# A two-layer trunk on one core: the first feed-forward block by seven half-size products, with the S5 tables made in small pieces

## The chip, the cores and the metric

The kernel runs on one core of a Trainium2 chip. The metric is the device time of one execution in microseconds (us), the median of several runs. Engines are named as in the profile: PE multiplies matrices (PEld loads its weights), DVE does elementwise work, ACT does functions and copies, POOL is the fourth compute engine and also issues transfers of its own, SP only issues transfers.

## What is computed

Two layers over 544 tokens (512 of a prompt and 32 of samples) of width 1024. Each layer is a gated feed-forward block, a set of four mixers (SSD, RWKV, S5, pool) between an input and an output projection, and a second gated feed-forward block; a last norm follows.

```python
def _layer(x, pos0, st, p):
    x = x + 0.5 * _swiglu(_rmsnorm(x, p['norm_ffn1']), p['ffn1_in'], p['ffn1_out'])
    u = _rmsnorm(x, p['norm_mix']) @ p['w_in']
    ...                                    # four mixers on slices of u
    x = x + y @ p['w_out']
    x = x + 0.5 * _swiglu(_rmsnorm(x, p['norm_ffn2']), p['ffn2_in'], p['ffn2_out'])
```

The S5 mixer needs `a_bar = exp(lam*delta)`, its powers, and products of these powers with `b` and `c`; they depend on the weights alone and are called the S5 tables here.

## The kernel before

**Layout.** x lies in SBUF as eight tiles of 128 channels by 544 tokens, and is worked on in two halves of 272 tokens. Weights come from DRAM in chunks of eight 128x128 blocks (`fetch`, tile `wraw`, four buffers). Every fp32 value is split in a rounded high part and the rest, so a product of one weight block with one tile is six matmuls of 272 columns (`mm3`, L832 to L834: high by high, high by low, low by high, for two halves). The weight split is `parts` (L816 the cast on ACT, L819 the subtraction on DVE); its results `whi` and `wlo` have three buffers of four blocks each.

**The feed-forward block in two forms.** There are 22 hidden tiles m. In `ffn`, used for the first block of layer 0 alone, each hidden tile takes 16 weight blocks, that is 96 matmuls (`inph`); the output projection of a group of hidden tiles follows (`outph`, groups of 8, 8 and 6). In `ffs`, used for the three other blocks, the first four hidden tiles go the same way (`plain`); the other 18 go by `quad(m)`, which makes a 2x2 by 2x2 block product with seven instead of eight products of half-size (Winograd's scheme: 7 x 12 = 84 matmuls, L975 and L976). For this `forms` makes seven combinations of the normalized x once in a block, during `plain(1)` to `plain(3)`, and each quad makes its weight combinations t1 to t4 (L979, DVE), splits seven of them (`form`, tiles `xh0..7` and `xl0..7`; three of the seven low parts are made by a copy with the sign turned on ACT and an accumulating transfer issued by POOL, L818), and takes the four results out of PSUM (tiles `pm`, all four banks). Between quads lie two output tiles of the group before (`out`, PSUM tile `pd`, two buffers, evicted into x by L1007).

**The S5 tables.** `do_prep` runs `s5_prep` for both layers, as a generator whose next piece `ffn` asks for after each hidden tile from the third on. It has six pieces for each layer: two of small operations on 16 columns and one for each four of 16 S5 groups. A piece of four groups makes CA (three DVE operations, L593), GB (three), four transposes (L664) and four fp32 matmuls recorded as eight (L670) on PE with a PSUM bank of `pm`, two ACT copies, sines and cosines (`sincos`, L599 to L606) and RHO (two POOL operations), and writes the results to DRAM with 13 transfers on SP's queue (eight of them L673). The parameters come with one transfer on ACT's queue, tied behind the last weight fetch (`issue_after`).

**Order.** The program is traced in the order of the code, and a scheduler at compile time then puts each engine's instructions in a fixed order, the earliest traced first among those that it holds ready. Work traced later can so fill gaps of work traced earlier. In `ffn` weights are fetched by ACT's queue, in `ffs` by SP's.

**Constants.** One tile `cst` with all constants is loaded at the start by SP, and `mat`, weights of the mixers, by ACT at the start of each layer (L1199).

Of the kernel before, what the change touches and what calls it, by code (L numbers as in the profile page):

```python
# [7 lines left out]
def build_consts():  # L8
    c={}
    I=np.arange  # L10
    p=I(128)
# [93 lines left out]
class Mix:  # L105
# [6 lines left out]
    def c(s,n,rows=128):  # L112
        o,k=CC[n]; return s.cst[0:rows,o:o+k]
# [3 lines left out]
    def load_consts(s,cst):  # L117
        s.cst=s.const.tile([128,CONST.shape[1]],F32,name="cst"); s.nc.sync.dma_start(s.cst,cst)
# [463 lines left out]
    def s5_prep(s,par,name,tp):  # L582
# [5 lines left out]
        tl=lambda n,a: tp.tile([128]+a,F32,name=n)  # L588
# [8 lines left out]
        def sincos(E,y,sn,cs,k):  # L597
# [30 lines left out]
        bbr=tl("bbr",[16,16]); bbi=tl("bbi",[16,16]); t3=tl("t3",[16,16]); bbS=tl("bbS",[16,16])  # L628
        qrb=qr[:,:,None].to_broadcast([128,16,16]); qib=qi[:,:,None].to_broadcast([128,16,16])
        TT(V,bbr,br,qrb,M); TT(V,t3,bi,qib,M); TT(V,bbr,bbr,t3,SB)  # L630
        TT(V,bbi,bi,qrb,M); TT(V,t3,br,qib,M); TT(V,bbi,bbi,t3,AD)
        A.copy(bbS[0:64],bbr[0:64]); A.copy(bbS[64:128],bbi[64:128])

        A1=tl("A1",[9,16]); A2=tl("A2",[9,16])
        V.tensor_copy(A1[0:64],pr[0:64]); V.tensor_copy(A1[64:128],pi[64:128])
        V.tensor_copy(A2[0:64],pi[0:64]); V.tensor_copy(A2[64:128],pr[64:128])
        sg=s.c('sgn')
# [4 lines left out]
        ab4=tl("ab4",[32]); V.tensor_copy(ab4[:,0:16],pr[:,4,:]); V.tensor_scalar(ab4[:,16:32],pi[:,4,:],sg,-1.0,op0=M,op1=M)  # L642
# [8 lines left out]
        for g0 in range(0,16,4):  # L651
# [10 lines left out]
            GT=tl("GT",[4,128])  # L662
            ps=s.bank(); pv=ps.rearrange("p (g q) -> p g q",g=4)
# [5 lines left out]
            ps=s.bank(); pv=ps[0:16,:].rearrange("p (g q) -> p g q",g=4)  # L669
# [4 lines left out]
            ph=tl("ph",[4,64]); kk=tl("kk5",[4,64]); SN=tl("SN",[4,64]); CS=tl("CSt",[4,64])  # L674
# [3 lines left out]
            V.tensor_scalar(SN,SN,sg,None,op0=M)  # L678
# [87 lines left out]
GROUPS=[list(range(0,8)),list(range(8,16)),list(range(16,22))]  # L766
# [18 lines left out]
class Kern(Mix):  # L785
    def __init__(s,tc,nc,ctx,io):
        Mix.__init__(s,tc,nc,ctx)
        s.io=io
        s.fi=0
        s.wp=s.P("wp",3); s.xhl=s.P("xhl",1); s.hole=ExitStack()  # L790
        s.wi=0; s.lo=nc.vector; s.dq=nc.scalar
        s.psm=s.P("psm",4,space=bass.MemoryType.PSUM,reuse_waits="tile"); s.psd=s.P("psd",2,space=bass.MemoryType.PSUM,reuse_waits="tile")
# [86 lines left out]
    def ffn(s,st,gnext,bg=iter(())):  # L879
        nc=s.nc  # L880
        with s.tc.tile_pool(name="ffh",bufs=12,reuse_waits="tile") as hp, s.tc.tile_pool(name="fft",bufs=2,reuse_waits="tile") as tp, s.tc.tile_pool(name="ffr",bufs=1,reuse_waits="tile") as rp:
            r=None; hs={}
            v2=lambda t: t.rearrange("p (a b) -> p a b",a=2)
            def inph(m):
                nonlocal r
                pg=s.psd.tile([128,2,512],F32,name="pd")
# [292 lines left out]
    def run(s):  # L1179
# [15 lines left out]
        st={}  # L1195
# [112 lines left out]
```

## Time and profile before

| | |
|---|---|
| median of 3 runs | 2282.89 us (2279.74 to 2290.09) |
| profiled execution, time | 2284.78 us |
| profiled execution, span | 2283.0 us |
| PE busy | 2182.9 us, 96% |
| DVE, ACT, POOL busy | 65%, 48%, 24% |

The profile is that of one execution. A line names the engine, the source line, the tiles written and read, and the duration; what stands in brackets is how long the engine had been idle before and what ended that. The stages follow one another: first feed-forward block of layer 0 to 444 us, mixers to 785, second block to 1163, first block of layer 1 to 1545, mixers to 1889, second block to the end.

### The profile page before, as it was taken

Reading aid. Unit: us, or ns where it says so; the run is one execution under the profiler, and the core shown is the slowest. Engines: PE = TensorE matmul, PEld = TensorE weight load, DVE = VectorE, ACT = ScalarE, POOL = GpSimd, SP = SyncE. Lnnn points to the kernel's source line nnn. Section 1 sums busy time; section 2 is a strip of 40 time slices with the busy share of each in tenths; the row PEclk is TensorE's granted clock in tenths of the full one; section 3 lists DMA queues with packets and bytes.
Section 4 is the critical chain, followed back from the end, with each engine's and each line's share of the span. In section 5 each row is a group of like instructions: output and inputs, shape, how many; then the busy total and the mean of one; then the engine's idle time right before and its main releaser. Section 6 shows DMA issues by size and latency. Waiting matters only on the chain. (4 is left out here: it accounts for less than half of the span.)

```text
span 2283.0 us, 42463 instructions
## 1 busy us (share of the span) xinstructions
PE 2182.9 (96%) x16838; PEld 2124.7 (93%) x16838; DVE 1486.7 (65%) x2757; ACT 1093.6 (48%) x2008; POOL 556.6 (24%) x636
## 2 busy tenths in 40 slices
PE   7899999989899999999999999999899999999997
PEld 7899999988789999999999999999777999999997
DVE  7848633458876677666567666653877667766664
ACT  5324322445435465555455555544554446555542
POOL 3311201334322231111122111114433133111112
PEclk9999999999999999999999999999999999999999
DMA  4343522443322265555437555544432144656551
GB/s 178 114 121 110 147 91 86 150 148 103 101 69 88 86 153 153 140 152 134 116 94 174 133 148 144 139 132 155 118 102 74 36 131 115 174 130 159 129 145 51
DMA packets 142198, 281.20 MB, mean 123 GB/s; under 512 B 36144, under 2 KB 60720, under 8 KB 141872
## 3 DMA queue, kind: packets, MB, share of 16 engines
q1 hardware_dynamic: 91520, 150.77, 20.2%
q0 software_dynamic: 26784, 49.16, 12.6%
q10 hardware_dynamic: 23696, 78.56, 10.5%
q8 instruction: 132, 2.16, 0.4%
q14 instruction: 66, 0.54, 0.1%
HBM read 201.07 MB, written 28.22 MB: 100 GB/s over the span
## 5 line engine op out<-in xcount | busy, mean ns | idle before, releaser
L832 PE MATMUL pd<-xh,whi 128*128 128x272 f32 (+1 forms) x1984 | 548.3, 295 | 17.7 <-ACT whi L816 10.7
L833 PE MATMUL pd<-xl,whi 128*128 128x272 f32 (+1 forms) x1984 | 553.9, 295 | 3.6 <-DVE xl L850 3.5
L816 ACT CAST whi<-wraw 128x512 fp32r<-128x512 f32 x428 | 263.6, 618 | 519.0 <-PE pd L833 405.0
L834 PE MATMUL pd<-xh,wlo 128*128 128x272 f32 (+1 forms) x1984 | 423.7, 294 | 17.0 <-DVE wlo L819 15.2
L832 PEld LDWEIGHTS pd<-xh,whi 128*128 128x128 f32 x1984 | 381.7, 192 | 23.7 <-ACT whi L816 11.9
L975 PE MATMUL pm<-AH,xh 128*128 128x272 f32 x1512 | 393.6, 288 | 5.9 <-DVE e L979 4.2
L975 PE MATMUL pm<-AL,xh 128*128 128x272 f32 x1512 | 393.2, 288 | 0.0
L833 PEld LDWEIGHTS pd<-xl,whi 128*128 128x128 f32 x1984 | 382.5, 193 | 8.2 <-DVE xl L850 5.1
L832 PE MATMUL pd<-hh,whi 128*128 128x272 f32 x1396 | 376.4, 288 | 0.0
L833 PE MATMUL pd<-hl,whi 128*128 128x272 f32 x1396 | 375.9, 288 | 0.0
L834 PEld LDWEIGHTS pd<-xh,wlo 128*128 128x128 f32 x1984 | 322.4, 192 | 22.5 <-DVE wlo L819 18.5
L819 DVE TENSOR_TENSOR wlo<-wraw,whi 128x512 fp32r<-128x512 f32 x328 | 239.0, 729 | 119.8 <-ACT whi L816 113.4
L975 PEld LDWEIGHTS pm<-AH,xh 128*128 128x128 f32 x1512 | 284.4, 188 | 7.2 <-DVE e L979 4.9
L834 PE MATMUL pd<-hh,wlo 128*128 128x272 f32 x1396 | 288.7, 288 | 0.0
L975 PEld LDWEIGHTS pm<-AL,xh 128*128 128x128 f32 x1512 | 284.6, 188 | 0.0
L833 PEld LDWEIGHTS pd<-hl,whi 128*128 128x128 f32 x1396 | 262.8, 188 | 0.0
L832 PEld LDWEIGHTS pd<-hh,whi 128*128 128x128 f32 x1396 | 262.7, 188 | 0.0
L818 POOL DMA_DIRECT2D xl<-wraw x108 | 93.7, 867 | 654.8 <-DVE s L979 443.4
L976 PE MATMUL pm<-AH,xl 128*128 128x272 f32 x1512 | 252.1, 288 | 0.2 <-DMA xl<-sqa 0.2
L834 PEld LDWEIGHTS pd<-hh,wlo 128*128 128x128 f32 x1396 | 219.1, 188 | 0.0
L976 PEld LDWEIGHTS pm<-AH,xl 128*128 128x128 f32 x1512 | 214.9, 188 | 0.4 <-DMA xl<-sqa 0.4
L819 POOL TENSOR_TENSOR wlo<-wraw,whi 128x512 fp32r<-128x512 f32 x100 | 137.0, 1375 | 158.8 <-ACT whi L816 129.9
(516 smaller groups left out, 3316.1 us busy)
## 6 DMA issues: line engine op xcount, KB each, us to landing
wraw<-in_w SPq DMA_DIRECT2D x198, 512.0 KB, 4.0
wraw<-in_w ACTq DMA_DIRECT2D x124, 512.0 KB, 3.4
xl<-wraw POOLq DMA_DIRECT2D x108, 256.0 KB, 3.6
xl<-sqa POOLq DMA_DIRECT2D x54, 256.0 KB, 3.3
AL<-ss POOLq DMA_DIRECT2D x24, 272.0 KB, 5.2
xd<-x SPq DMA_DIRECT2D x16, 272.0 KB, 2.9
x<-xd SPq DMA_DIRECT2D x16, 272.0 KB, 4.7
x<-in_x SPq DMA_DIRECT2D x8, 272.0 KB, 6.9
```

The lines of the kernel that those rows point to most:

```text
L816: nc.scalar.copy(hi,x)
L818: nc.scalar.mul(lo,x,-1.0); nc.gpsimd.dma_start(lo,x,accum_op=OP.add)
L819: else: s.lo.tensor_tensor(lo,x,hi.bitcast(F32),op=OP.subtract)
L832: nc.tensor.matmul(p,wh,rh[:,a:b],start=(n==0),stop=False)
L833: nc.tensor.matmul(p,wh,rl[:,a:b],start=False,stop=False)
L834: for p,a,b in o: nc.tensor.matmul(p,wl,rh[:,a:b],start=False,stop=(n==K-1))
L975: for t in F[j]: nc.tensor.matmul(o,wh[:,j,:],t[:,f,:],start=first and j==0 and t is F[j][0],stop=False,skip_group_check=True)
L976: for j in range(4): nc.tensor.matmul(o,wl[:,j,:],F[j][0][:,f,:],start=False,stop=j==3,skip_group_check=True)
```

## The change

The function `ffn` is dropped, and the first block goes by `ffs` too, so that 18 of its 22 hidden tiles are quads. `s5_prep` is cut into 15 pieces for each layer; layer 0's tables are made in the first block, layer 1's in the second block of layer 0, one piece asked for after each quad. In a piece, small multiplications and copies go from DVE to ACT, the PSUM tile is of `pd`, and several tiles lie in buffers of the feed-forward block (`ss`). The constants are in two tiles: a small one loaded at the start, and a large one that is loaded, like `mat`, at the start of each layer's mixers, into memory that the feed-forward block has used for its `gt`, `s2` and `e`. The hidden tiles have 8 buffers instead of 9 in `ffs` (12 in `ffn`). x lies on the other side of SBUF in the first block.

```diff
+    c['nsg']=-c['sgn']
+    c['hpi']=np.full((128,1),math.pi/2,np.float32)
...
-            V.scalar_tensor_tensor(k,y,-1.0,y,op0=M,op1=OP.max)
-            E.tensor_scalar(k,k,-1.0,math.pi/2,op0=M,op1=AD)
-            A.activation(cs,k,AF.Sin)
+            A.activation(k,y,AF.Abs)
+            A.activation(cs,k,AF.Sin,scale=-1.0,bias=s.c('hpi'))
...
+        yield dst
...
-        V.tensor_scalar(P1,A1,sg,None,op0=M); V.tensor_scalar(P2,A2,-1.0,None,op0=M)
+        A.mul(P1,A1,sg); A.mul(P2,A2,-1.0)
         for d in range(8):
-            V.tensor_copy(Q1[:,7-d,:],A1[:,d,:]); V.tensor_scalar(Q2[:,7-d,:],A2[:,d,:],sg,-1.0,op0=M,op1=M)
+            A.copy(Q1[:,7-d,:],A1[:,d,:]); A.mul(Q2[:,7-d,:],A2[:,d,:],ng)
...
-            GB=tl("GB",[4,8,16]); u=t4[:,:,0:8,:]
+            yield dst
+            GB=half(("p (g s c) -> p g s c",dict(g=4,s=8))); u=t4[:,:,0:8,:]
...
-            ps=s.bank(); pv=ps.rearrange("p (g q) -> p g q",g=4)
+            pp=s.psd.tile([128,2,512],F32,name="pd"); pv=pp[:,0,:].rearrange("p (g q) -> p g q",g=4)
...
-            ph=tl("ph",[4,64]); kk=tl("kk5",[4,64]); SN=tl("SN",[4,64]); CS=tl("CSt",[4,64])
+            yield dst
+            pk,sc=[half(("p (a g k) -> p a g k",dict(a=2,g=4))) for _ in range(2)]; ...
...
-            V.tensor_scalar(SN,SN,sg,None,op0=M)
+            A.mul(SN,SN,sg)
...
-    def ffn(s,st,gnext,bg=iter(())):
...
-    def ffs(s,st,gcur,gnext):
+    def ffs(s,st,gcur,gnext,bg=iter(())):
...
-            ...; hp=pool("ffh",9); tp=pool("fft",2); rp=pool("ffr",1)
+            ...; tp=pool("fft",2); rp=pool("ffr",1); hp=pool("ffh",8)
...
-                for k in range(KD): s.mm3(pg,st[k],k,KD,s.HALF)
-                if r is None: r=s.rstd(st['acc'],rp,tp,'gt')
+                for k in range(KD):
+                    if k not in st: st[k]=s.split(k,s.x[k],s.v(gcur,k))
+                    s.mm3(pg,st[k],k,KD,s.HALF)
+                if 'acc' not in st:
+                    with s.tc.tile_pool(name="ini",...) as ip: s.squares(st,ip); r=s.rstd(st['acc'],rp,tp,'gt')
+                elif r is None: r=s.rstd(st['acc'],rp,tp,'gt')
...
-                    quad(m)
+                    quad(m); next(bg,None)
                     for M in out_order(gi,q): out(SGROUPS[gi-1],M,False)
+            for _ in bg: pass
...
+        mx=s.hole=ExitStack(); rk=ExitStack(); mc=pool(mx,"mxc")
+        s.load_consts(1,mc); s.mat=mc.tile([128,1024],F32,name="mat"); nc.sync.dma_start(s.mat,io['mat'][l][:,0:1024])
         for k in range(KD): nc.sync.dma_start(xd[k],s.x[k])
-        s.xctx.close(); s.hole.close()
+        s.xctx.close()
...
-        s.open_x()
+        s.open_x("right")
...
-        s.load_consts(io['cst'])
-        s.mat=s.const.tile([128,1024],F32,name="mat"); ...
+        s.load_consts(0,s.const)
...
-            nc.scalar.dma_start(s.mat,io['mat'][l][:,0:1024])
...
-            st=s.ffn(st,'nm',s.do_prep()) if l==0 else s.ffs(st,'nf1','nm')
+            st=s.ffs(st,'nf1','nm',s.do_prep(0) if l==0 else iter(()))
...
-        r=s.ffs(st,'nf2','nf1'); s.norm_tile=old
+        r=s.ffs(st,'nf2','nf1',s.do_prep(1)); s.norm_tile=old
```

## Rows read from the trace of the kernel before

**Rows 1.** The page, part 1: busy times, shares of the span, instructions.
```profile
PE 2182.9 (96%) x16838; PEld 2124.7 (93%) x16838; DVE 1486.7 (65%) x2757; ACT 1093.6 (48%) x2008; POOL 556.6 (24%) x636
```

**Rows 2.** DVE's timeline (start us, us, line, operation): evictions that mark pitches.
```profile
390.23 0.73 DVE L897 TENSOR_TENSOR gt<-pd,rsq_r 128x544 f32<-128x544 f32 x1 [1.92 <-PE pd L834]
402.29 0.72 DVE L897 TENSOR_TENSOR gt<-pd,rsq_r 128x544 f32<-128x544 f32 x1 [1.92 <-PE pd L834]
...
1109.10 0.44 DVE L979 TENSOR_TENSOR e<-pm,e 128x272 f32<-128x272 f32 x1 [0.73 <-PE pm L976]
1119.67 0.44 DVE L979 TENSOR_TENSOR e<-pm,e 128x272 f32<-128x272 f32 x1 [0.39 <-PE pm L976]
```

**Rows 3.** DVE's timeline: the last eviction of each stage into x.
```profile
444.47 0.72 DVE L912 SCALAR_TENSOR_TENSOR x<-pd,x 128x544 f32<-128x544 f32 x1 [2.19 <-PE pd L834]
785.68 0.72 DVE L1122 TENSOR_TENSOR x<-pd,x 128x544 f32<-128x544 f32 x1
1163.28 0.72 DVE L1007 SCALAR_TENSOR_TENSOR x<-pd,x 128x544 f32<-128x544 f32 x1 [0.40 <-PE pd L834]
1544.77 0.72 DVE L1007 SCALAR_TENSOR_TENSOR x<-pd,x 128x544 f32<-128x544 f32 x1 [2.19 <-PE pd L834]
1889.43 0.72 DVE L1122 TENSOR_TENSOR x<-pd,x 128x544 f32<-128x544 f32 x1
```

**Rows 4.** PE's timeline: the first block's second hidden tile begins.
```profile
34.24 0.36 PE L832 MATMUL pd<-xh,whi 128*128 128x272 f32 x1 [1.91 <-DVE gt L897]
```

**Rows 5.** Stretches of the first block: busy time (count) of PE, PEld, DVE, ACT, POOL; clock; DMA.
```profile
25.00:125.00 100.00, 92.13 (x688) 89.55 (x687) 80.23 (x194) 39.44 (x72) 28.81 (x25) 0.96 0.38 118
175.00:275.00 100.00, 99.39 (x786) 97.19 (x786) 80.60 (x194) 40.15 (x71) 23.24 (x22) 1.00 0.43 133
300.00:400.00 100.00, 100.00 (x799) 100.00 (x798) 33.90 (x51) 26.56 (x43) 12.21 (x9) 1.00 0.26 87
55.00:65.00 10.00, 8.15 (x53) 7.93 (x52) 10.00 (x35) 3.93 (x7) 2.69 (x2) 0.83 0.39 125
```

**Rows 6.** What PE waited for from 25 to 126 us: total, times, longest.
```profile
PE pd L834 <- DVE wlo L819: 6.0, 4, 2.1
```

**Rows 7.** PE's timeline around the tables' transposes and matmuls of four groups.
```profile
87.18 0.60 PE L664 MATMUL pm<-cst,GB 128*128 128x128 f32 x4
87.71 1.05 PE L670 MATMUL pm<-CA,bbS 128*16 128x128 f32 x8
88.68 0.39 PE L832 MATMUL pd<-xh,whi 128*128 128x272 f32 x1
```

**Rows 8.** PE's waits, 862 to 1163 us (all) and 1230 to 1550 us (all).
```profile
PE pm L975 <- DVE e L979: 0.8, 1, 0.8
...
PE pm L975 <- DVE e L979: 2.2, 1, 2.2
```

**Rows 9.** Stretches of the second block of layer 0, columns as in rows 5.
```profile
829.00:845.50 16.50, 16.50 (x133) 16.50 (x133) 16.00 (x26) 13.59 (x26) 5.58 (x6) 1.00 0.83 201
862.00:1079.00 217.00, 216.24 (x1722) 216.01 (x1721) 145.09 (x253) 114.71 (x211) 33.68 (x39) 1.00 0.56 143
```

**Rows 10.** ACT's timeline in that block: a cast just after a quad's first product.
```profile
1057.20 0.62 ACT L816 CAST xh<-sq 128x512 fp32r<-128x512 f32 x1 [0.16 <-PE pm L975]
```

**Rows 11.** Table operations: timeline at 97 us; durations (min/median/max ns) of three.
```profile
97.78 1.40 POOL L903 TENSOR_TENSOR hl<-s,hh 128x544 fp32r<-128x544 f32 x1
97.88 1.91 DVE L593 TENSOR_TENSOR CA<-CA,t 128x576 f32<-128x576 f32 x1
...
L593 DVE TENSOR_TENSOR CA<-s5par,P x8: 744/1916/1925, 58.8 to 262.4; 128x576 f32<-128x576 f32 x8
L606 ACT ACTIVATE cs<-kr x4: 198/200/218, 44.2 to 205.4; 128x16 f32<-128x16 f32 x4
L673 SPq DMA_DIRECT2D s5d<-KZ x64: 313/424/1725, 98.3 to 279.4; - x64
```

**Rows 12.** The accumulating transfers of the quads: durations of issue on POOL.
```profile
L818 POOL DMA_DIRECT2D xl<-wraw x108: 855/862/1022, 839.1 to 2219.8; - x108
```

More of the change, by code (lines that the diff above doesn't have):

```diff
@@ L45, in build_consts @@
     c['rcnt']=(1.0/np.minimum(I(16)[None,None,:]+1,w[:,:,None])).astype(np.float32).reshape(128,32)
-    cols={}; o=0; arr=[]
+    c['nsg']=-c['sgn']
+    c['hpi']=np.full((128,1),math.pi/2,np.float32)
+    cols={}; arr=[[],[]]
     for n,a in c.items():
-        cols[n]=(o,a.shape[1]); o+=a.shape[1]; arr.append(a)
-    return np.ascontiguousarray(np.concatenate(arr,1)),cols
+        j=0 if n in ('idn','one','kap','sgn','nsg','hpi') else 1
+        cols[n]=(j,sum(b.shape[1] for b in arr[j]),a.shape[1]); arr[j].append(a)
+    return [np.ascontiguousarray(np.concatenate(a,1)) for a in arr],cols
 F32=mybir.dt.float32; F32R=mybir.dt.float32r
@@ L112, in c @@
     def c(s,n,rows=128):
-        o,k=CC[n]; return s.cst[0:rows,o:o+k]
+        j,o,k=CC[n]; return s.cst[j][0:rows,o:o+k]
     def v(s,n,j=0,k=1):
@@ L587, in s5_prep @@
         dst=s.dram.tile([128,O['END']],F32,name=name)
-        tl=lambda n,a: tp.tile([128]+a,F32,name=n)
+        tl=lambda n,a,tag=None: tp.tile([128]+a,F32,name=n,tag=tag or n)
+        half=lambda a: s.ntp.tile([128,T],F32,name="ss",bufs=2)[:,0:512].rearrange(a[0],**a[1])
         pt=tl("s5par",[1072])
@@ L673, in s5_prep @@
                 nc.sync.dma_start(dst[si*16:si*16+16,g0*128:g0*128+512].rearrange("p (g q) -> p g q",g=4),KZ[:,:,128-16*si:256-16*si])
-            ph=tl("ph",[4,64]); kk=tl("kk5",[4,64]); SN=tl("SN",[4,64]); CS=tl("CSt",[4,64])
+            yield dst
+            pk,sc=[half(("p (a g k) -> p a g k",dict(a=2,g=4))) for _ in range(2)]; ph,kk,SN,CS=pk[:,0],pk[:,1],sc[:,0],sc[:,1]
             kap=s.c('kap')[:,None,:].to_broadcast([128,4,64])
@@ L1191, in run @@
         s.pre.append(s.fetch(1))
-        s.load_consts(io['cst'])
-        s.mat=s.const.tile([128,1024],F32,name="mat"); s.om=s.const.tile([128,12],F32,name="om")
+        s.load_consts(0,s.const)
+        s.om=s.const.tile([128,12],F32,name="om")
         s.vec=s.vecs[0]
@@ L1207, in run, with do_prep @@
             st=s.ffn2(l,st)
-        s.xctx.close(); s.hole.close()
-    def do_prep(s):
+        s.xctx.close()
+    def do_prep(s,l):
         with s.tc.tile_pool(name="s5prep",bufs=1,side="right",reuse_waits="tile") as tp:
-            for l in range(2):
-                for s.prep[l] in s.s5_prep(s.io['s5par'][l],f"s5d{l}",tp): yield
+            for s.prep[l] in s.s5_prep(s.io['s5par'][l],f"s5d{l}",tp): yield
     def ffn2(s,l,st):
@@ L1238, in ffs @@
             for h in SGROUPS[-1]: out.append(blk(wo,h,M))
-    def ffn(wi,wo):
-        def inb(m):
-            for k in range(8): out.append(blk(wi,k,m))
-            for k in range(8): out.append(blk(wi,k,m+NH))
-        for gi,G in enumerate(GROUPS):
-            for m in (G if gi==0 else G[1:]): inb(m)
-            if gi<2: inb(GROUPS[gi+1][0])
-            for M in range(8):
-                for m in G: out.append(blk(wo,m,M))
-    (ffs if l else ffn)(i['ffn1_in'][l],i['ffn1_out'][l])
+    ffs(i['ffn1_in'][l],i['ffn1_out'][l])
     W=i['w_in'][l]
```

75 lines of the change are left out of this document (19 added, 56 removed).

## The prediction

> **What bounds the kernel now.** I read the page's first part, then the stages, then each stage's waits. PE is busy for 96% of the span, no other engine for more than 65% [rows 1]. That is a share over stages, so I looked for the pitch of the work. In the first block's later part one hidden tile's half is evicted at 390.23 us and the next tile's at 402.29, so a plain hidden tile takes 12.06 us for 96 matmuls, 0.1256 us each; where two quads follow each other without output tiles between them, their evictions stand 10.57 us apart, which is 84 matmuls at 0.1258 us [rows 2]. Both pitches are those of matmuls with no gap. The blocks are thus bounded by the number of matmuls, with exceptions in the first block: from 25 to 125 us PE is busy for 92.13 of 100 us, and it had 688 matmuls where a quiet stretch of the same block has 799 [rows 5]. There DVE is full (10.00 of 10 us from 55 to 65 us), the granted clock falls to 0.83 of full speed, a mixture of 2.4 and 1.2 GHz, after PE had waited [rows 5], and PE waits for the low parts of weights, four times, 6.0 us in all [rows 6]. What fills DVE there are the S5 tables.
>
> **The change part by part.** The profiled execution took 2284.78 us with a span of 2283.0; the median of the runs is 2282.89. I make the sum on the trace and take it off the median, which is 1.9 us below the profiled time.
>
> *Seven products.* 18 hidden tiles go from 12.06 to 10.57 us: 18 x 1.49 = **-26.8 us** [rows 2]. The output projection has the same 1056 matmuls before and after. This is on the path, since PE has no gap at either pitch.
>
> *What the tables cost in the old first block.* PE begins the second hidden tile at 34.24 us [rows 4] and the last eviction is at 444.47 [rows 3], 410.2 us. The matmuls in it are 22 x 96 + 1056 - 96 = 3072, at 0.1256 us 385.8 us. The tables' own PE work of four groups lasts from 87.18 to 88.68 us, 1.5 us [rows 7], and there are eight such, 12.0 us. The remainder is 410.2 - 385.8 - 12.0 = 12.4 us. The 6.0 us of waits are half of it [rows 6]; a clock of 0.83 over 10 us is another 1.7 us, and the like once more around 100 us. All of it goes with the old arrangement: **-12.4 us**. The 12.0 us of table work stay, half of them moved from the first block to the second: 0.
>
> *What the form with seven products costs by itself.* A block of this form has 4 x 96 + 18 x 84 + 1056 = 2952 matmuls, at 0.1256 us 370.8 us. The second block of layer 0 takes 1163.28 - 785.68 = 377.6 us, the first of layer 1 381.5 us [rows 3], so 6.8 and 10.7 us more. Most of that is the norm at the start, which the old first block has too, before 34.24 us; after the start I find waits of 0.8 us in one and of 2.2 us in the other [rows 8]. I take **+3 us**, between 0.8 and 6.
>
> *The tables between the quads.* This is the term that no row shows. The demand first. While layer 1's tables were made, DVE was busy 80.60 us in 100; without tables 33.90 [rows 5]. The tables of a layer thus cost DVE about 47 us. In the quads' stretch DVE is busy 145.09 us of 217, ACT 114.71 [rows 9]; a quad and two output tiles last 10.57 + 6.03 = 16.6 us, so DVE is free for 5.5 us of each and ACT for 7.8. There are 16 such pairs in a block, 88 us of free DVE time for 47 us of tables, in pieces of some 2 to 4 us. Less than 47 will be wanted: of each layer's operations on 16 columns some 18 go to ACT at about 0.2 us (the like of L606's 198 ns), 3.6 us, and ACT has 16 x 7.8 = 125 us [rows 9, 11].
>
> Then the slack. In the old block the low parts of weights have three buffers, each good for 24 matmuls or 3.0 us, so one is made at most 6.0 us before its use. In a quad the cast at 1057.20 us waited for PE to leave the tile that the quad's first product had read [rows 10]. There are eight such tiles and seven forms in a quad, so this cast is for the second product of the *next* quad, which begins 16.6 us later. A piece of 2 to 4 us on DVE does not reach PE through the forms. The tight ones are the evictions of `pm`: a bank is needed again two products, 3.0 us, after its product ends. An eviction can stand behind one table operation of 0.7 to 1.9 us, not behind a whole piece.
>
> First what the row shows on the length of these operations: the CA operations took 744 ns at best and 1916 at the median, and one of 1.91 us at 97.88 us stands beside a POOL subtraction of 1.40 us that began 0.1 us before it [rows 11]. The Trainium skill (SBUF — State Buffer, SBUF: two separate sides) has the port pair that VectorE and GpSimd share as an exclusive lock: whoever comes first holds it for its whole instruction. The trace agrees, 1.91 us against 0.744. By that rule the tables would be cheaper in quads, where the subtraction and the last product are DVE's own: 4 x (1.916 - 0.744) = 4.7 us of each layer's 47 would go for the first CA operation alone. The sum below does not use it.
>
> The price: at best 0 (below that, the remainder of 12.4 us has already been taken off in full). At worst as much for each piece as in the old block, 12.4 us over 12 pieces, 1.03 us, times 30 new pieces: 31 us. I take **+7 us**, near the lower end, because the lead is nearly three times as long and the old loss fell almost wholly on layer 0: PE was 99.39% busy while layer 1's tables were made [rows 5]. Part of it I expect around the fourth hidden tile, where DVE is already busy 16.00 of 16.5 us [rows 9] and the first pieces come.
>
> *Queues.* The tables' 53 transfers of a layer now share SP's queue with the weight chunks, which ACT's queue had in the old first block. Eight of them at 0.42 us stand in a row [rows 11], 3.4 us in which a chunk can wait; the lead of a quad hides that. Without it, 8 x 3.4 = 27 us; I take 0. The parameters' load was tied behind a weight fetch on ACT's queue and is so no longer; it can only come earlier. SP's load of the large constants waits for tiles last read by the last quad; behind it on SP stand x's stores, which wait for the last output tiles (36 us of matmuls) anyway: 0.
>
> *Start.* The norm's matmuls come after the eighth instead of the ninth weight block, so the factor is known up to 1.5 us sooner, and PE had waited 1.91 us for it at 34.24 [rows 4]: **-1 us**, between -1.9 and 0.
>
> *Mixers.* In layer 0 they take 785.68 - 444.47 = 341.2 us, in layer 1, where x already lay on the side that it now has in layer 0 too, 344.7 us [rows 3]: **+2 us**, between 0 and 3.5. Eight hidden buffers: outputs of a group are done one quad before the ninth is needed: 0.
>
> Sum: -26.8 - 12.4 + 3 + 7 - 1 + 2 = **-28.2 us**, so 2282.9 - 28.2 = 2254.7, say **2255 us**.
>
> **The rivals.**
>
> *Tables cost per piece what they did* (31 us for 7): -4.2, **2279 us**. For it: the schedule is fixed at compile time and DVE went full in the old block with only 34% other work [rows 5]; quads have 67% [rows 9]. Against: the longer lead [rows 10].
>
> *Tables cost nothing*, and the start gains in full: -26.8 - 12.4 + 0.8 - 1.9 = -40, **2243 us**. For it: 0.6 us lost in 100 with layer 1's tables.
>
> *Evictions behind pieces: slower.* If the order puts a whole piece, not one operation, ahead of a `pm` eviction, PE stops each time, and the clock falls as at 55 us. A stop of 2.1 us [rows 6] with 1.7 us of lower clock is 3.8 us; over the 24 group pieces 91 us in place of 7: **2339 us**. It decides from 46 us in all, 12 such stops: more than three table operations in a row on DVE while a bank is wanted. Against: 10.57 us pitches hold in a DVE that is 67% full.
>
> *Scattered pieces don't stay where they are put.* The scheduler may draw the first pieces into the four plain hidden tiles, where the lead is 6 us, and DVE makes the forms. Then each layer has a stretch like 25 to 125 us, which holds the remainder of 12.4 us but for the 0.6 lost with layer 1's tables [rows 5]; 11.8 us in each of two blocks in place of 7: **2271 us**.
>
> *Accumulations starved.* The issues of POOL take 0.86 us, at most 1.02 [rows 12]. If each of the 108 in two blocks were held by 1 us, PE would lose only where the lead of about 10 us is gone; one stop of 2 us in each of the first three quads gives +12, **2267 us**. The Trainium skill (SBUF — State Buffer, SBUF: two separate sides) warns that a two-port VectorE operation locks GpSimd out and starves transfers issued from it; no run here shows tables beside such issues.
>
> **How the numbers follow.** Forecast 2255 with its terms' smaller errors: 0.56. Tables free: 0.12. Pieces in the plain tiles: 0.10. Accumulations starved: 0.03. Per-piece cost as before: 0.12. Evictions behind pieces, slower: 0.07. About 0.5%, 11.4 us, is what a measurement of this kernel can tell from no change, so faster begins at 2271.5. The first, second and fourth case and half of the third are faster, 0.76, and with the lower part of the per-piece case 0.78; the rest of these two are same: 0.15; slower 0.07. The range goes from the tables-free case, 2243, to 2272, which leaves out the per-piece case and the slower one.
>
> **What would show it.** Right: in the first block, quad evictions 16.6 us apart as in the second, PE over 97% busy from 40 us on, its last eviction at about 404 us instead of 444.47; second block some 9 us longer; DVE at 80 to 88% in quads; clock at 1.00 except at the start. Wrong: waits of PE for `e` or `s` with a clock under 0.9 in the quads (slower); waits for `wlo` between 34 and 75 us (pieces drawn early); `xl` from transfers as a reason (accumulations); mixers more than 4 us longer.

## The result

The changed kernel takes 2254.98 us (median of 4 runs, 2249.87 to 2255.82), the kernel before beside it 2283.43: a ratio of 0.987, interval 0.984 to 0.9895. The forecast was 2255. The two profiled executions (spans 2283.0 and 2252.4 us) differ by 30.6 us.

The page of the changed kernel, part 1 (busy time, share of the span, instructions):

```profile
PE 2154.5 (96%) x16622; PEld 2095.6 (93%) x16622; DVE 1553.4 (69%) x2891; ACT 1190.7 (53%) x2247; POOL 552.1 (25%) x658
```

Beside [rows 1], PE has 216 matmuls fewer, 18 hidden tiles by 12, and DVE more work in a shorter span. PE's timeline at the first matmul and at the second hidden tile answers to [rows 4]:

```profile
6.53 0.59 PE L839 MATMUL pd<-xh,whi 128*128 128x272 f32 x1 [6.53 <-ACT whi L823]
30.76 0.36 PE L839 MATMUL pd<-xh,whi 128*128 128x272 f32 x1 [0.52 <-ACT whi L823]
```

DVE's timeline, the last eviction of each stage into `x`, answers to [rows 3]:

```profile
403.18 0.72 DVE L978 SCALAR_TENSOR_TENSOR x<-pd,x 128x544 f32<-128x544 f32 x1 [2.17 <-PE pd L841]
749.53 0.72 DVE L1096 TENSOR_TENSOR x<-pd,x 128x544 f32<-128x544 f32 x1
1137.24 0.72 DVE L978 SCALAR_TENSOR_TENSOR x<-pd,x 128x544 f32<-128x544 f32 x1 [0.40 <-PE pd L841]
1517.07 0.72 DVE L978 SCALAR_TENSOR_TENSOR x<-pd,x 128x544 f32<-128x544 f32 x1 [2.17 <-PE pd L841]
1858.64 0.71 DVE L1096 TENSOR_TENSOR x<-pd,x 128x544 f32<-128x544 f32 x1
```

| stage | before, us | after, us | difference |
|---|---|---|---|
| first block | 444.5 | 403.2 | -41.3 |
| mixers of layer 0 | 341.2 | 346.4 | +5.1 |
| second block of layer 0 | 377.6 | 387.7 | +10.1 |
| first block of layer 1 | 381.5 | 379.8 | -1.7 |
| mixers of layer 1 | 344.7 | 341.6 | -3.1 |
| rest | 393.6 | 393.8 | +0.2 |

The last eviction of the first block, expected at about 404 us, comes at 403.18, and the second block, expected to be about 9 us longer, is 10.1 longer. Stretches of the changed kernel (busy time and count of PE, PEld, DVE, ACT, POOL; granted clock; DMA share; GB/s), first of block 1, then around the start of layer 0's second block:

```profile
30.00:50.00 20.00, 18.76 (x147) 18.35 (x147) 17.39 (x30) 13.95 (x25) 8.01 (x6) 1.00 0.43 112
50.00:75.00 25.00, 22.60 (x173) 21.72 (x173) 19.90 (x46) 18.62 (x33) 7.72 (x8) 1.00 0.59 142
75.00:100.00 25.00, 23.81 (x187) 23.38 (x187) 24.15 (x69) 23.25 (x62) 4.83 (x6) 1.00 0.72 175
100.00:125.00 25.00, 24.22 (x193) 24.00 (x192) 22.28 (x42) 13.02 (x28) 4.33 (x5) 1.00 0.77 197
125.00:400.00 275.00, 275.00 (x2190) 273.16 (x2190) 188.09 (x332) 145.12 (x272) 51.78 (x59) 1.00 0.59 158
sum 370.00, PE 364.39 PEld 360.60 DVE 271.81 ACT 213.95 POOL 76.67; mean PE 72.88 PEld 72.12 DVE 54.36 ACT 42.79 POOL 15.34
...
785.00:795.00 10.00, 6.46 (x40) 5.80 (x40) 9.63 (x22) 7.96 (x14) 3.31 (x4) 0.85 0.46 109
795.00:805.00 10.00, 10.00 (x67) 10.00 (x67) 9.26 (x36) 5.86 (x11) 1.58 (x3) 0.80 0.67 162
830.00:1080.00 250.00, 250.00 (x1991) 248.16 (x1990) 184.39 (x333) 137.28 (x260) 46.22 (x56) 1.00 0.62 160
```

From 125 us on, PE has no gap at all while the tables are made, at a clock of 1.00; DVE is 68% busy there. What is lost in the first block lies before 125 us: 3.6 us from 30 to 75 (the plain tiles, where the forms are made) and 2.0 from 75 to 125 (the first table pieces). In the second block most of the loss lies between 785 and 805 us: PE stops three times, and the clock is 0.85 and 0.80 in the two halves, a mixture of 2.4 and 1.2 GHz. Around the longest of these stops DVE's, POOL's and PE's timelines show:

```profile
789.58 1.48 DVE L597 TENSOR_TENSOR t<-pi,s5par 128x16 f32<-128x16 f32 x1
789.51 1.50 POOL L931 TENSOR_TENSOR s<-gt,rsq_r 128x544 f32<-128x544 f32 x1
792.95 0.82 PE L841 MATMUL pd<-xh,wlo 128*128 128x272 f32 x2 [1.71 <-DVE wlo L826]
```

The first line is a table operation on 16 columns that was drawn into the plain tiles. It took 1.48 us, until POOL's product ended, and the low part of a weight for which PE waited (792.22 to 792.90) stood behind it on DVE.

### The profile page after: what moved, and what is told of

Same layout as the page of the kernel before. It is cut to its first block, busy times and chain, and to the rows that moved or that the text cites. A ratio compares the mean times of both kernels' runs of the same rounds, so it can differ in the third digit from the quotient of the medians.

```text
span 2252.4 us, 42511 instructions
## 1 busy us (share of the span) xinstructions
PE 2154.5 (96%) x16622; PEld 2095.6 (93%) x16622; DVE 1553.4 (69%) x2891; ACT 1190.7 (53%) x2247; POOL 552.1 (25%) x658
## 5 line engine op out<-in xcount | busy, mean ns | idle before, releaser
L946 PE MATMUL pm<-AH,xh 128*128 128x272 f32 x2016 | 524.8, 289 | 6.1 <-DVE e L950 3.2
L946 PE MATMUL pm<-AL,xh 128*128 128x272 f32 x2016 | 523.7, 288 | 0.0
L839 PE MATMUL pd<-xh,whi 128*128 128x272 f32 (+2 forms) x1408 | 392.1, 297 | 16.5 <-ACT whi L823 10.9
L840 PE MATMUL pd<-xl,whi 128*128 128x272 f32 (+2 forms) x1408 | 396.7, 297 | 3.2 <-DVE xl L857 3.2
L946 PEld LDWEIGHTS pm<-AH,xh 128*128 128x128 f32 x2016 | 379.0, 188 | 8.1 <-DVE e L950 4.1
L946 PEld LDWEIGHTS pm<-AL,xh 128*128 128x128 f32 x2016 | 378.8, 188 | 0.0
L841 PE MATMUL pd<-xh,wlo 128*128 128x272 f32 (+2 forms) x1408 | 305.8, 297 | 14.9 <-DVE wlo L826 11.9
L839 PEld LDWEIGHTS pd<-xh,whi 128*128 128x128 f32 x1408 | 272.6, 194 | 21.8 <-ACT whi L823 12.3
L840 PEld LDWEIGHTS pd<-xl,whi 128*128 128x128 f32 x1408 | 272.7, 194 | 8.0 <-DVE xl L857 5.0
L841 PEld LDWEIGHTS pd<-xh,wlo 128*128 128x128 f32 x1408 | 231.6, 193 | 19.2 <-DVE wlo L826 14.2
L978 DVE SCALAR_TENSOR_TENSOR x<-pd,x 128x544 f32<-128x544 f32 x159 | 114.6, 721 | 97.9 <-PE pd L841 97.6
```

The source lines that it names most:

```text
L839: nc.tensor.matmul(p,wh,rh[:,a:b],start=(n==0),stop=False)
L840: nc.tensor.matmul(p,wh,rl[:,a:b],start=False,stop=False)
L841: for p,a,b in o: nc.tensor.matmul(p,wl,rh[:,a:b],start=False,stop=(n==K-1))
L946: for t in F[j]: nc.tensor.matmul(o,wh[:,j,:],t[:,f,:],start=first and j==0 and t is F[j][0],stop=False,skip_group_check=True)
L978: V.scalar_tensor_tensor(xv,po[:,:,:H],0.5,xv,op0=OP.mult,op1=OP.add)
```

## The experiments

All are compared with the changed kernel's 2255.0 and the kernel before's 2283 to 2285 us. A stage "ends" with its last eviction into `x`.

**e1 and e2: the tables left out.** The S5 tables' computation is left out; zeros are written in place of them. e1 does that in the kernel before, e2 in the changed one.

```diff
-            for s.prep[l] in s.s5_prep(s.io['s5par'][l],f"s5d{l}",tp): yield
+            for s.prep[l] in s.no_tables(f"s5d{l}",tp): yield
+        z=tp.tile([128,1156],F32,name="zt"); nc.gpsimd.memset(z,0.0)
+        for i in range(8): nc.sync.dma_start(dst[:,i*1156:i*1156+1156],z)
```

> The kernel before without the computation of the S5 tables: zeros of the same size are written to the tables' place instead, so the S5 mixer computes with zeros. Theory (the first block loses 12.4 us to the tables beyond their 12.0 us of PE work): 2283 - 24.4 = 2259 us, and PE 99% busy or more from 40 to 440 us. Rival (that loss belongs to the block's start and not to the tables): only the 12 us go, 2271 us.

Measured: 2259.94 us, ratio 0.989 (0.986 to 0.992), as the theory has it. Block 1 is 26.4 us shorter. Of that, 2.1 us is a second hidden tile that begins sooner, which is not the tables' doing (see e11). PE's timeline of e1 at its first matmul and where its second hidden tile begins:

```profile
7.34 0.59 PE L832 MATMUL pd<-xh,whi 128*128 128x272 f32 x1 [7.34 <-ACT whi L816]
32.10 0.36 PE L832 MATMUL pd<-xh,whi 128*128 128x272 f32 x1 [1.91 <-DVE gt L897]
```

A stretch of e1, columns as above:

```profile
125.00:400.00 275.00, 275.00 (x2192) 275.00 (x2192) 95.37 (x141) 77.80 (x124) 40.02 (x30) 1.00 0.27 90
```

Its first block ends at 418.06 us, 386.0 after the second tile; the prediction's 3072 matmuls at 0.1256 us are 385.8. So without tables the old block loses nothing: the 12.4 us of remainder were the tables'.

> The changed kernel without the computation of the S5 tables, zeros in their place as in the run beside it. Theory (tables cost 12 us of PE work and 4 to 8 us of stalls between the quads): 2255 - 19 = 2236 us, 2233 to 2240; against the kernel before without tables that is the price of the seven products alone, 27 us less 3 to 5. Rival (tables cost nothing but their PE work): 2243 us. Rival (a stall for each of the 30 pieces as in the old block, 31 us): 2212 us.

Measured: 2245.15 us, ratio 0.9825 (0.9805 to 0.9845). The theory's 2236 fell. Block 1 ended at 399.2 us because PE stopped in the plain tiles. PE's and DVE's timelines of e2, with the idle time and its releaser in brackets:

```profile
45.69 0.44 DVE L896 TENSOR_TENSOR ss<-sq 128x272 f32<-128x272 f32 x1 [4.41 <-DMA AL<-ss]
...
57.01 0.82 PE L841 MATMUL pd<-xh,wlo 128*128 128x272 f32 x2 [3.54 <-DVE wlo L826]
```

PE waits for the low part of a weight, but DVE, which makes it, stands idle: its next operation in order writes a form's sum into the tile `ss`, and that has two buffers which the accumulating transfers of the tile before (`AL<-ss`) still read. The low part stands behind it in DVE's queue. In e2 the zeros were written at just that time, so e9 and e12 ask whether the kernel or my zeros made the stop.

**e9 and e12: the zeros moved.** The tables' computation is left out in both, as in e2. e9 puts one transfer of zeros after each of eight quads in the program; e12, whose diff is shown, also ties each behind a weight fetch, and e9 has that line without the tie.

```diff
-        for i in range(8): nc.sync.dma_start(dst[:,i*1156:i*1156+1156],z)
+        for i in range(8):
+            yield dst
+            with s.tc.issue_after(s.fetched): nc.sync.dma_start(dst[:,i*1156:i*1156+1156],z)
```

> The changed kernel without the S5 tables, as e2, but the zeros that stand in their place are written one 578 KB transfer after each of eight quads, not all together at 27 to 50 us. The tables' computation is left out. In e2 DVE stood 9.7 us for the release of the tile ss by accumulating transfers AL<-ss, which took 8.0 us each to land instead of 4.8, while the zeros were written. Theory that e2's stop in the plain tiles (PE waits for wlo of 6.5 us, clock 0.86) came from its own transfers: AL<-ss lands in about 5 us, PE has no wait over 2 us for wlo, block 1 ends at 391 to 395 us, not at 399.2, and the time is 2234 to 2241 us; the tables then cost the changed kernel 14 to 20 us, close to the sum's 12 on PE plus 7. Rival, that the forms stop the plain tiles by themselves: 2243 to 2247 us as e2.

Measured: 2244.01 us (2243.33 to 2245.2). This edit missed its aim: a transfer of zeros waits for nothing, so it was scheduled at 25.6 to 49 us as before, and e9 is e2 again.

> e9 again, with the one thing mended that it missed: in e9 the zeros that stand for the tables were still written at 25 to 50 us, because they waited for nothing; here each of these transfers is tied behind the weight fetches of its quad. The orders of PE, DVE and POOL are those of e9 line for line, so only the place of the transfers differs. The tables' computation is left out. Theory that e2's and e9's stops in the plain tiles come from their own transfers (AL<-ss landed in 6 us and DVE stood 9.6 us for it): AL<-ss lands in under 5 us, DVE waits for ss under 6 us and PE for wlo under 3 us in 28:80, block 1 ends 4 to 7 us sooner than e9's 400.73, and the time is 2234 to 2241 us; the tables then cost the changed kernel 14 to 20 us, next to the sum's 12 + 7. Rival, that the forms stop the plain tiles by themselves: block 1 ends at 399 to 401 us and the time is 2242 to 2247 us; the tables then cost 10 to 11 us in all, no more than their own PE work.

Measured: 2246.47 us (2244.65 to 2247.82). DVE's longest wait from 28 to 80 us (total, times, longest) in e9, in e12 and in the changed kernel, one fence each:

```profile
DVE ss L896 <- DMA AL<-ss: 9.6, 3, 4.3
```

```profile
DVE ss L896 <- DMA AL<-ss: 5.5, 3, 2.7
```

```profile
DVE ss L896 <- DMA AL<-ss: 4.6, 3, 2.0
```

And stretches of e9 (first fence) and e12 (second):

```profile
30.00:50.00 20.00, 16.01 (x127) 15.79 (x126) 12.90 (x24) 9.96 (x19) 6.33 (x5) 0.99 0.73 226
50.00:75.00 25.00, 21.85 (x152) 21.62 (x152) 19.70 (x34) 15.62 (x31) 8.36 (x8) 0.87 0.72 176
```

```profile
30.00:50.00 20.00, 18.80 (x148) 18.36 (x146) 16.35 (x29) 13.63 (x25) 7.88 (x6) 1.00 0.49 117
50.00:75.00 25.00, 22.48 (x177) 22.26 (x178) 19.54 (x34) 15.81 (x29) 9.45 (x9) 1.00 0.69 173
75.00:100.00 25.00, 21.31 (x164) 20.50 (x163) 18.41 (x33) 14.10 (x28) 4.28 (x5) 1.00 0.93 235
...
sum 370.00, PE 362.59 PEld 361.12 DVE 243.32 ACT 195.43 POOL 73.34; mean PE 72.52 PEld 72.22 DVE 48.66 ACT 39.09 POOL 14.67
```

The theory holds for the place and not for the total. With the zeros out of the way PE loses 3.7 us from 30 to 75 instead of 7.1, the changed kernel's own 3.6; so e2's stop there was half the experiment's doing. But the zeros now stand at 69 us and later, and from 75 to 100, where the DMA engines are 93% busy, PE loses 3.7 us (the changed kernel 1.2); that the zeros do it is likely and not shown. Block 1 ended at 397.62 us, 3.1 sooner than in e9, within neither bound, and the time is the rival's. By medians the tables thus cost 8.5 to 11 us, less than their 12 us of PE work; so what stands in their place costs some us itself. How much the tables cost in all is left between that and the 16 to 20 us that the rows of the changed kernel and of e7 give below.

**e3, e5 and e6: the table code.** e3 gives the changed kernel the old table code in two points: six large pieces a layer, and the small operations on DVE; the new buffers and the PSUM tile of `pd` stay. e5 takes back only the operations, e6 only the pieces. The operations are more than the 18 on 16 columns: six on 144 columns, four on 256 and the absolute values of `sincos` go back to DVE with them.

```diff
e3 and e6, at three places:
-            yield dst
e3 and e5, among others:
-        A.mul(P1,A1,sg); A.mul(P2,A2,-1.0)
+        V.tensor_scalar(P1,A1,sg,None,op0=M); V.tensor_scalar(P2,A2,-1.0,None,op0=M)
```

> The changed kernel with the tables' computation in six pieces a layer and with all its small operations on VectorE, as in the kernel before; still in the two blocks with quads. Theory (the quads' long lead absorbs the tables, whatever their pieces): 2255 us, 2252 to 2259. Rival (small pieces and the moves to ScalarE are what keeps the loss small): the loss of the old block, 12 us, in each of the two blocks, 2255 + 18 = 2273 us.

Measured: 2273.09 us, ratio 0.9947 (0.9926 to 0.9968): the rival's number, but not as the rival splits it. Block 1 is 14.2 us longer than in the changed kernel, ending at 417.39, the second block only 1.5. In block 1 PE's waits are 3.5 and 1.5 us for ACT's copies of the tables' own products (tiles `ss` and `KZ`), 2.1 for `wlo`, 1.6 each for `e` and `xl`, and 3.3 in one stop, the longest. DVE's and PE's timelines there:

```profile
102.66 0.69 DVE L948 TENSOR_TENSOR sqa<-wraw,sq 128x512 f32<-128x512 f32 x1 [2.19 <-DMA xl<-sqa]
102.68 1.27 PE L945 MATMUL pm<-AH,xl 128*128 128x272 f32 x4 [3.31 <-DMA xl<-sqa]
```

The stretch around it, and then the transfers issued from 96 to 104 us (count, KB each, median us to landing):

```profile
100.00:125.00 25.00, 22.32 (x157) 22.32 (x158) 18.59 (x32) 12.90 (x26) 4.33 (x5) 0.86 0.63 155
```

```profile
wraw<-in_w SPq DMA_DIRECT2D x2, 512.0 KB, 5.3
xl<-sqa POOLq DMA_DIRECT2D x1, 256.0 KB, 6.6
```

An accumulating transfer that lands in 3.5 us in the median of the changed kernel's page took 6.6 here, beside two weight chunks; PE stood 3.31 us for it and DVE 2.19, and the clock over these 25 us is 0.86. So a transfer of POOL did stop a quad, as the prediction's rival of starved accumulations had it, but POOL's issues were not longer, and why it landed late no run shows.

> The changed kernel, with one thing of the table code undone: some 18 operations on 16 columns of each layer, which the change gives to ACT, stand on DVE again, as in the kernel before. The pieces stay small (fifteen groups a layer). With the old code whole (e3: these operations on DVE and six large pieces) the kernel took 2273 us, 18 us more than the changed kernel. Theory of the engine (DVE is the scarce one, and each operation on it delays evictions and forms): most of the 18 us is here, 2265 to 2273 us, with DVE over 85% busy in the quads that have pieces. Theory of the piece size (a large piece delays what stands behind it, whatever engine): 2255 to 2259 us here, and the loss in e6.

Measured: 2255.73 us (2253.33 to 2257.18), not to be told from the changed kernel's time. DVE is 24.16 of 25 us busy from 100 to 125 us, and PE waits for `e` in block 1 six times, 3.9 us in all instead of 1.7, and little more. Theory of the engine: fell, as far as DVE alone goes.

> The changed kernel, with the other thing undone: three of the places where the table code lets the hidden tiles go on are taken out, so that the groups' first pieces are joined to six large ones a layer; the operations given to ACT stay there. Theory of the piece size: most of the 18 us of e3 is here, 2265 to 2273 us, with stops of PE for a form's or an eviction's tile (wlo, e) of 2 to 3 us and a granted clock under 0.95 where the large pieces stand, 75 to 150 us. Theory of the engine: 2255 to 2259 us.

Measured: 2261.55 us (2261.39 to 2265.99), so 6.6 us for the size of the pieces: between the two theories. No wait of PE in block 1 was over 1.8 us, nor was the clock under 1.00 from 75 to 150. In the profiled execution the two blocks with tables are 3.8 and 1.8 us longer than in the changed kernel, and more than that lies in stages that the edit does not touch. Alone the two parts cost 0.8 us, which is within the noise, and 6.6, together 18.1: they count mainly together. By which wait they do so no run isolates; e3's waits are spread over the tables' own copies, weights and evictions.

**e4: the parameters.** The tables' parameters are loaded on SP's queue, tied behind a weight fetch, in place of ACT's queue, to keep the first pieces out of the plain tiles.

```diff
-        with s.tc.issue_after(s.fetched): A.dma_start(pt,par)
+        with s.tc.issue_after(s.fetched): nc.sync.dma_start(pt,par)
```

> The changed kernel with the table parameters loaded on SyncE's queue, tied behind the weight fetch of the first quad, so that no table operation can run in the four plain hidden tiles. Theory (the first pieces, drawn into the plain tiles, make the stop and the lower clock from 790 to 800 us in the second block, some 4 us): 2251 us, with that stretch at a clock of 1.00. Rival (the stop there comes from the forms of x): 2255 us and the same stretch at a clock of 0.66.

Measured: 2259.0 us (2256.66 to 2261.55), 4 us more than the changed kernel. In the second block the first table operation now comes at 795.76 us, and there is still a stop: PE 6.83 of 10 us from 785 to 795 at a clock of 0.93, beside 6.46 at 0.85. But it is another one. DVE's timeline of e4:

```profile
792.44 0.44 DVE L896 TENSOR_TENSOR ss<-sq 128x272 f32<-128x272 f32 x1 [4.46 <-DMA AL<-ss]
```

DVE stood idle for an accumulating transfer, the weight's low part behind it, and PE waited 3.17 us for that. The parameters, 536 KB, were issued at 785.4 us, so they were on their way at just that time; from 776 to 800 us `AL<-ss` took 6.0 us to land (median; the changed kernel's 5.1). As with e2's zeros, the edit put a transfer of its own beside those of the forms, so e4 does not decide between its two theories.

**e7: room in the quads.** The tables of both layers are made in block 1, two pieces after each quad.

```diff
-                    quad(m); next(bg,None)
+                    quad(m); next(bg,None); next(bg,None)
-            st=s.ffs(st,'nf1','nm',s.do_prep(0) if l==0 else iter(()))
+            st=s.ffs(st,'nf1','nm',(y for q in (0,1) for y in s.do_prep(q)) if l==0 else iter(()))
```

> The changed kernel, but the tables of both layers are made in the first block, two pieces after each quad in place of one, and none in the second. Same work in all. The prediction had no row on how much room the quads have. Theory that the quads have room (DVE was 76% busy in them with one piece): PE still has no gap, the first block gets longer by the tables' 12 us on PE alone, the second shorter by the same and by the stop at its start: 2248 to 2256 us. Rival, that two pieces fill DVE as the old block did (67% plus twice 9 to 15%): DVE over 95%, waits of PE for e, clock under 0.95 in 100 to 250 us, and 2265 to 2285 us.

Measured: 2262.72 us (2262.23 to 2268.98), between the two. Block 1 ends at 420.02, 16.8 us later for 6 us of PE work; its second tile began 0.9 us later. A stretch of e7, and then the largest of PE's waits from 30 to 404 us (total, times, longest):

```profile
200.00:250.00 50.00, 47.92 (x383) 47.71 (x381) 41.44 (x119) 39.77 (x93) 9.77 (x12) 1.00 0.59 163
```

```profile
PE pd L676 <- ACT ss L671: 3.4, 3, 2.4
```

DVE was at 83%, not full, and still PE lost 2 us in 50: it stood for the copies of the tables' own transposed blocks by ACT. Two pieces do not fill DVE, but PE then meets the tables' own chain more often.

e7 also shows a second block of the changed arrangement with neither tables nor zeros in it. DVE's timeline, the last evictions of layer 0's mixers and of that block:

```profile
762.85 0.72 DVE L1096 TENSOR_TENSOR x<-pd,x 128x544 f32<-128x544 f32 x1
1142.97 0.72 DVE L978 SCALAR_TENSOR_TENSOR x<-pd,x 128x544 f32<-128x544 f32 x1 [0.40 <-PE pd L841]
```

It takes 380.1 us, against 387.7 with layer 1's tables and 377.6 in the kernel before.

**e8: the low part of a hidden tile on POOL.**

```diff
-                A.copy(hh,x); V.tensor_tensor(hl,x,hh.bitcast(F32),op=OP.subtract)
+                A.copy(hh,x); nc.gpsimd.tensor_tensor(hl,x,hh.bitcast(F32),op=OP.subtract)
```

> The changed kernel, with the subtraction that gives a hidden tile's low part moved from DVE to POOL in the tiles that had it on DVE. It tests the one citation of the prediction: that table operations on DVE are long (1.9 us in place of 0.75) where POOL's subtractions run, and that issues of POOL's transfers suffer. Theory that the two hold each other up: the CA operations go from a median of 747 ns back toward 1.4 to 1.9 us, the issues on POOL get longer than 0.9 us, and the time is 2260 to 2280 us in spite of DVE having less to do. Rival, that they don't: CA stays at 0.75 us, DVE is some 3% less busy, and the time is 2252 to 2257 us.

Measured: 2264.6 us (2259.6 to 2268.22): the time of the first theory, by another operation than it named. The CA operations stayed at 746 ns in the median; none met a POOL subtraction. Others did. POOL's and DVE's operations on e8's timeline, a 16-column operation at 64.92 and a `wlo` at 35.53 behind POOL subtractions that were running, and one that reads PSUM at 111.48:

```profile
35.39 1.45 POOL L914 TENSOR_TENSOR hl<-s,hh 128x544 fp32r<-128x544 f32 x1 [1.52 <-ACT hh L914]
35.53 1.86 DVE L826 TENSOR_TENSOR wlo<-wraw,whi 128x512 fp32r<-128x512 f32 x1
...
63.97 2.28 POOL L914 TENSOR_TENSOR hl<-s,hh 128x544 fp32r<-128x544 f32 x1 [0.20 <-ACT hh L914]
64.92 1.35 DVE L597 TENSOR_TENSOR pr<-er,cs 128x16 f32<-128x16 f32 x1
66.20 0.17 DVE L597 TENSOR_TENSOR pi<-er,sn 128x16 f32<-128x16 f32 x1
...
111.11 1.36 POOL L914 TENSOR_TENSOR hl<-s,hh 128x544 fp32r<-128x544 f32 x1 [3.10 <-ACT hh L914]
111.48 0.72 DVE L978 SCALAR_TENSOR_TENSOR x<-pd,x 128x544 f32<-128x544 f32 x1 [0.54 <-PE pd L841]
```

PE paid for it at 83.07 us, where it waited 2.29 us for `e` after a 16-column operation that took 1.36 us in the same way; the clock from 75 to 125 is 0.93. The hold-ups are shown; that they make up the whole 9.6 us is not.

**e10: the forms' sums in two tile names.**

```diff
-            sa,sb=[s.ntp.tile([128,T],F32,name="ss",bufs=2) for _ in range(2)]
+            sa,sb=[s.ntp.tile([128,T],F32,name="ss" if j%2==0 else "sqa",bufs=2) for _ in range(2)]
```

> The changed kernel, where the sums of the forms of tiles 1 and 3 lie in the tile name sqa, which is idle then, in place of ss: so DVE does not wait for the accumulating transfers of the tile before to have read ss. Same arithmetic. In the changed kernel's four blocks DVE waits 5.5, 2.2, 6.1 and 6.7 us for that release, with the operations on the low parts of weights queued behind it. Theory that this wait is what costs the plain tiles: these waits fall under 2 us in each block, PE gains 1 to 3 us in each, and the time is 2243 to 2251 us. Rival, that DVE's or ACT's amount of work in these tiles is the limit (DVE busy 5.0 of 5 us in 30:40): the waits go to another operation, and the time is 2252 to 2257 us.

Measured: 2253.25 us (2248.24 to 2255.68), ratio 0.9865 (0.9846 to 0.9883) beside the change's 0.987: not to be told from it. The wait for `ss` is gone, and 1.4 to 1.7 us are left for `sqa` in each of three blocks. What PE waits for instead is a quad's first `xh` or `xl` (3.3 us in the second block, 2.7 in the first), and from 30 to 75 us it is busy for 40.8 us, the changed kernel for 41.4; DVE is full there:

```profile
30.00:50.00 20.00, 19.01 (x149) 18.82 (x150) 20.00 (x35) 15.04 (x27) 9.98 (x6) 1.00 0.52 121
50.00:75.00 25.00, 21.81 (x160) 21.37 (x160) 23.47 (x74) 19.87 (x36) 10.39 (x7) 0.92 0.58 129
```

That fits the rival: in these tiles the amount of work on DVE and ACT is the limit, and the wait for `ss` was only its first sign. Part of DVE's full time is no work, though: a form's sum at 32.55 us took 1.59 us in place of 0.43 while POOL multiplied.

**e11: the start.** The kernel before, with the load of the mixers' matrices moved from ACT's queue to SP's.

```diff
-            nc.scalar.dma_start(s.mat,io['mat'][l][:,0:1024])
+            nc.sync.dma_start(s.mat,io['mat'][l][:,0:1024])
```

> The kernel before, with one load moved: the mixers' matrices are loaded from SP's queue in place of ACT's, where that issue stood ahead of the cast of the first x tile. It asks where the 3.5 us come from by which the changed kernel's second hidden tile begins sooner (the prediction had -1). Theory that ACT's queue held the start: first matmul at 6.5 to 7.0 us in place of 8.45, and the second hidden tile begins about 1.9 us sooner than 34.24. Rival, that the start is set by the arrival of x: first matmul stays at 8.2 to 8.6 us.

Measured: a single run of 2290.07 us. ACT's and PE's timelines of e11:

```profile
4.86 0.75 ACT L850 ACTIVATE xh<-x,vec 128x544 fp32r<-128x544 f32 x1 [2.18 <-DVE vec L1185]
6.73 0.59 PE L832 MATMUL pd<-xh,whi 128*128 128x272 f32 x1 [6.73 <-ACT whi L816]
32.02 0.36 PE L832 MATMUL pd<-xh,whi 128*128 128x272 f32 x1 [1.91 <-DVE gt L897]
```

The theory's numbers came: first matmul 1.7 us sooner, the second tile 2.2 us sooner, at 32.02 against 34.24 [rows 4]. But the load does not explain them. e1 leaves it on ACT's queue and begins its second tile at 32.10. The first chunk of weights landed at 6.83 us in the profile of the kernel before, at 5.76 in e1 and at 6.04 in e11; the first matmul followed 1.6 us later in the first two and 0.7 us later in e11. So the load costs 0.9 us at the first matmul, of which nothing is to be seen at the second tile of e1, and the rest is when the chunk landed. That differs from one execution to the next: 5.84 us in the changed kernel, 7.64 in e7. The total of a single run says nothing on 2 us.

## Why the prediction was right

**Seven products, -26.8: right.** The 216 matmuls are gone from the page, and from 125 to 400 us 2190 matmuls take 275.00 us, 0.1256 each: PE is bound by their number, as at the pitches of [rows 2]. Quads with tables between them stand as far apart as forecast (16.6 us); two `e` evictions on DVE's timeline of the changed kernel:

```profile
281.19 0.44 DVE L950 TENSOR_TENSOR e<-pm,e 128x272 f32<-128x272 f32 x1
...
297.75 0.44 DVE L950 TENSOR_TENSOR e<-pm,e 128x272 f32<-128x272 f32 x1 [0.73 <-PE pm L947]
```

**The old block's loss, -12.4: right,** shown by e1, whose block has just the time of its matmuls.

**The form's own cost, +3: right.** PE loses 3.6 us between 30 and 75 us, and 3.7 in e12 without tables. As to why, e10 points to DVE and ACT, which have more to do than these tiles have time for.

**The tables between the quads, +7: the upper part of what was found.** In block 1, 403.18 - 30.76 = 372.4 us passed after the second tile began; 2856 matmuls are 358.7 us, the tables' PE work 6.0, and 7.7 are left where the sum had 3 + 3.5. Of these, 3.6 are the form's, 2.0 fall between 75 and 125 us, and 2.1 are not seen as a gap in any stretch. The second block got 10.1 us longer, of which 6.0 is PE's work and 4.1 the rest; against e7's second block without tables it is 7.6, and 1.6 are left. So 2.0 to 4.1 in the first and 1.6 to 4.1 in the second: 3.6 to 8.2 in all, where the sum had 7. That part of it comes from the first pieces around the fourth hidden tile was expected, and there is one such stop, that of 792.95 us. So the rival of pieces that do not stay where they are put came true, but in small: it had 11.8 us for each block, and 2271 in all. No run shows the block with those pieces away and nothing else moved: e4 put a load there, and e9 and e12 zeros. After 830 us the tables cost no gap at all: PE 250.00 of 250.

The demand was put too high: a layer's tables took not 47 us of DVE but 28.5, the difference of the two sums from 30 to 400 us above (271.81 and 243.32). DVE is thus 68% busy from 125 to 400 us and 74% from 830 to 1080, not 80 to 88; only where the first pieces come, from 75 to 125, is it at 93%. About 4 us of the difference are the operations given to ACT (e5: 275.78 us in the same stretch), close to the 3.6 expected, though that counted only the 18 on 16 columns. Another part is the first CA operation, which the sum left out: eight of them at 748 ns each in place of a median of 1916 [rows 11].

```profile
L597 DVE TENSOR_TENSOR CA<-s5par,P x8: 748/748/758, 91.5 to 991.3; 128x576 f32<-128x576 f32 x8
```

The prediction took 4.7 us of a layer for it, as if all were at the median. Three of the eight had been short already (744 to 758 ns), two of layer 0's four and one of layer 1's, so it is 2.3 us for layer 0 and 3.5 for layer 1. The Trainium skill (SBUF — State Buffer, SBUF: two separate sides) let one expect shorter operations once the subtraction and the last product are DVE's own; the trace agrees, 748 against 1916 ns. The other 10 us or so of the difference no run accounts for. On the end it did not count where PE has no gap.

**Which part of the new table code does it:** the prediction took the small pieces and the moves to ACT for granted, and rested its +7 on the lead of 16.6 us. e3 shows that the lead is not enough: with the old code in those two points the time is 2273, near the rival with the cost per piece as before, 2279. A loss of that size was thus real for the old pieces, and the new ones avoid it.

**The start, -1 with -1.9 as its end: too small.** The second tile begins 3.5 us sooner, at 30.76. The norm sooner is part of it: PE's wait for `gt` of 1.91 is gone, and 0.52 for a weight's high part is left, 1.4 us. The other 2 us the prediction did not see. The load of the mixers' matrices, which the change moves, stood on ACT's queue in front of the first `xh`, but it explains at most 0.9 (e11); 1.0 is a first weight chunk that landed later in the profile of the kernel before, which is luck of that execution. In the eleven runs with the changed arrangement the second tile begins at 29.2 to 31.6 us.

**Mixers, +2: not settled.** Layer 0's are 5.1 us longer, past the 4 us that the prediction named as a sign of being wrong, and layer 1's 3.1 shorter. In the eleven runs with the changed arrangement, the changed kernel and its ten variants, layer 0's took 340.1 to 348.2 us, mean 344.4; in the three of the old one 341.2, 341.8 and 345.2. Layer 1's took 341.2 to 345.9, mean 343.2, against 344.7, 347.5 and 344.8. The means differ by +1.7 and -2.5, of the size of what one profile scatters. The profiled gain is 30.6 and not 28.2 because the first block gained 1.6 us more than forecast, layer 0's mixers lost 3.1 more, the second block 0.6 more, and the stages behind it gained 4.6, for which the sum had nothing. By the medians it is 28.4. The mechanism was right; that the median meets 2255 so closely is luck, with errors of some us both ways and runs that spread over 6 us.

**Queues and hidden buffers, 0: no loss found** in rows from 125 us on.

## What to carry to other kernels

Where one engine has no gap, count its instructions: the number of matmuls gave most of this result, and the rest had to be looked for only in the first 125 us and around one stop. Background work fits between two steps of a tight pipeline if each piece is short on the engine that also feeds the pipeline; split the piece first, and move small operations to another engine as well, since the two together were worth 18 us where each alone was worth under 7. And an experiment must not bring traffic of its own to the place that it asks about: zeros written at a bad moment (e2, e9) and a load moved there (e4) came with stops that hid what was asked.

## What the hardware showed

- DVE operations with two operands in SBUF that began while a POOL subtraction worked ended only after it. In e8 the 16-column one at 64.92 us took 1.35 us in place of 0.17 and ended at 66.27, POOL's at 66.25; the `wlo` at 35.53 ended 0.55 us after POOL's. In the changed kernel the one at 789.58 ended at 791.06, POOL's product at 791.01. One that reads PSUM kept its 0.72 us beside a POOL subtraction (e8, 111.48). The Trainium skill (SBUF — State Buffer, Who interferes with whom) names two SBUF inputs of a DVE instruction as what contends with a POOL instruction that reads SBUF; the trace agrees. The length of a DVE operation is no measure of what it can cost then: sixteen columns cost 1.35 us here, a whole tile 1.86.
- It works the other way too. The POOL subtraction at 63.97 us in e8 took 2.28 us in place of 1.36; DVE operations with two SBUF inputs ran until 65.0, the last of them begun inside POOL's record. The issue of accumulating transfers on POOL stayed at 0.86 us in the median in every kernel, with or without tables.
- What starved PE through accumulating transfers was their landing, not their issue: 6.6 us instead of 3.5 in e3, and 6.1 instead of 4.9 for `AL<-ss` where zeros were written beside them (e2, 28 to 60 us).
